# The gap between router and first expert of layer 0: rows scaled on ScalarE, shifts added at the copy out, first expert chunk ahead of a branch

## The chip, the cores and the metric

One core of a Trainium2 chip runs the whole program. The metric is the device time of one execution in microseconds (us). The kernel before takes 929.15 us (median of 3 runs, 928.97 to 929.91).

## The reference, cut to what matters

Two layers follow each other. Each has mixers (pooling, attention, a Fourier mix and an output projection), and after these a mixture of experts. The part that the change touches is the entry to the experts of layer 0, where 256 latent and 256 context tokens go through together:

```python
h2  = (rms_norm(x,  norm2_g[l]) * (1.0 + sc2) + sh2).reshape(B * N, D)
h2c = (rms_norm(xc, norm2_g[l]) * (1.0 + cs2) + ch2).reshape(B * L, D)
out = hier_moe(jnp.concatenate([h2, h2c], axis=0), *moe_args)

def hier_moe(h, w_grp, b_grp, w_rtr, b_rtr, w_gate, w_up, w_down):
    p_grp = softmax(h @ w_grp + b_grp);  pg, g = top_k(p_grp, 1)      # one of 4 groups
    logits = (h @ w_rtr + b_rtr) of that group
    pe, ie = top_k(softmax(logits), 2)                                # two of its 4 experts
    y = sum over experts e of gate[:, e] * (silu(h @ w_gate[e]) * (h @ w_up[e])) @ w_down[e]
```

The row scale of the norm (one number per token, `rs` below) multiplies a row, and the shift (`sh2` for latent, `ch2` for context tokens) is added to it. The factor (1 + scale) and the norm's weight are columns' factors and are in the tile `xt` already.

## The kernel before, in words

**Weights.** Nearly all DMA traffic is weights. `load` (L108) issues 2 MB transfers on SyncE's queue (SP) into a ring of five tiles and one further slot, in the order in which they are used. A load waits until TensorE (PE) has read the tile that it replaces. The experts are taken in four quads of four. For a quad, four chunks of `wg`, four of `wu` and then those of `wd` are used, 2 MB each.

**From the residual to the router.** When the last output projection is done, `Router` has the scaled residual transposed (L725) into `xt`: two tiles (halves of the 1024 columns) of 4 token tiles x 512. `rs` is the reciprocal of the root mean square (L278). `Route.choose` (L775 to L820) makes logits, top-1 and top-2 choices on VectorE (DVE), and counts the tokens of each expert with two sets of four small matmuls (L810, L812). `arrange` (L822 to L858) chooses the order of the quads and writes `plan`, a row of integers in which `more[q]` says whether an expert of quad q has more than 64 pairs. `slots` (L869 to L882) ends in `vec`, the two slot numbers of each token.

**Between the router and the experts.** `h2` (L745 to L752) scales each half row of `xt` by `rs` on ScalarE (ACT) and adds the shift, which stands in `room`, on GpSimd (POOL); seven of the eight half rows go that way, one is made on VectorE (L749). `split` (L115) makes of each half row a rounded part `h2h` (a cast on ScalarE) and the rest `h2l` (a subtraction on VectorE or GpSimd). Both halves of `xt` are written to DRAM (`h2d`, L1423, ScalarE's queue, 1 MB each); later quads fetch their rows from there (L1089, indirect DMAs on GpSimd's queue). `one_hots` (L1011 to L1020, pinned at L89) makes four 128x384 tiles, one for each token tile, with ones where a token's slot number is.

**Gather and branch.** `gather` (L1026 to L1044) multiplies `h2h` and `h2l` with the one-hots and so gets `XT`, the tokens of quad 0 by slot: 256 columns, 64 for each of four experts. The products are copied out by ScalarE and VectorE (L1040) in turn. Only then comes a branch (L1446) on `more[0]`, around a gather of 128 further columns for experts with more than 64 pairs. In these data it is not taken for quad 0. All engines read `plan` for it (L866). The first expert chunk (L1136) follows the branch. 8 matmuls belong to one chunk (two steps of four experts); the trace shows two records for most of them. Branches at L1146 stand around the columns beyond 64.

**Behind it.** VectorE makes diagonal tiles (`dg`, L287) which PE turns into rows that are the same on all partitions (`spread`, L288). ScalarE copies these out as `bc` and `bg` (L1162). From `bc` VectorE makes the slots' token lists (L1072 to L1084) and gates (L1122). GpSimd fetches rows of later quads by these lists. PE transposes them (L171), and ScalarE (L1102) or VectorE (L1104) copies the transposes into `XT`.

**Order.** Each engine takes its instructions in the order in which a list scheduler has laid them out from the written order; instructions marked as pinned keep the written order among themselves.

## Time and profile before

| | |
|---|---|
| median of 3 runs | 929.15 us (928.97 to 929.91) |
| the profiled execution | 929.26 us, span 927.4 us |
| PE busy | 865.7 us, 93% of the span |
| DVE, ACT, POOL busy | 409.9, 265.9, 64.5 us |
| mean DMA rate | 310 GB/s |
| mean granted PE clock | 0.979 of full speed |

PE is busy nearly all of the time and ends last, so that idle time of PE, or time at the lower of its two clocks, is what can be won. In the page's row of 40 slices PE's digits are 8 or 9 in nearly all slices behind the first; a 5 in the eleventh slice (231.9 to 255.0 us) is the largest hole. The granted clock, a row of nines, has a 6 in the same slice, an 8 further on and a 9 else. Times in the rows below are us from the start of the span. A row of a time line has start, duration, engine, line and what is written from what; a bracket at its end says how long the engine was idle before it and what ended that.

### The profile page before, as it was taken

How to read it: one execution, taken by the hardware profiler on the slowest of the kernel's cores; microseconds unless marked ns; L12 is line 12 of the kernel's file. 1: busy time of each engine (PE TensorE's matmuls, PEld its weight loads, DVE VectorE, ACT ScalarE, POOL GpSimd, SP SyncE). 2: the span in 40 equal slices, each digit the busy share in tenths (PEclk: the TensorE clock that was granted, in tenths of full speed). 3: DMA queues.
4: the chain of work that ended last, by engine and by line, in shares of the span. 5: the costliest groups of instructions: out<-in, count | busy, mean ns of one | idle time of the engine just before them, and what ended most of it. 6: DMA issues, size and time to landing. Idle time of an engine off the chain costs nothing. (4 is left out here: it accounts for less than half of the span.)

```text
span 927.4 us, 13199 instructions
## 1 busy us (share of the span) xinstructions
PE 865.7 (93%) x5078; PEld 478.1 (52%) x5078; DVE 409.9 (44%) x1028; ACT 265.9 (29%) x579; POOL 64.5 (7%) x74
## 2 busy tenths in 40 slices
PE   3899999999589999999999989989999999979998
PEld 2588676776353332442344357756973444434435
DVE  1467677633975230332221148877555241222212
ACT  3344667424320100110011055466422011100101
POOL 1000000001410030012000020000000000000000
PEclk9999999999699999999999998999999999989999
DMA  9645753744979999759958953985978999999981
GB/s 359 277 177 207 290 214 137 281 182 160 357 269 429 426 370 423 306 211 363 426 211 334 382 216 117 412 357 199 366 304 313 430 424 428 428 410 427 428 288 47
DMA packets 33826, 287.14 MB, mean 310 GB/s; under 512 B 3533, under 2 KB 13389, under 8 KB 17105
## 3 DMA queue, kind: packets, MB, share of 16 engines
q1 hardware_dynamic: 29168, 276.94, 74.3%
q0 software_dynamic: 1696, 5.79, 1.6%
q10 hardware_dynamic: 2880, 3.35, 1.0%
q8 instruction: 49, 0.80, 0.3%
q14 instruction: 33, 0.26, 0.1%
HBM read 282.90 MB, written 3.16 MB: 308 GB/s over the span
## 5 line engine op out<-in xcount | busy, mean ns | idle before, releaser
L1136 PE MATMUL acc<-w,XT 128*64 128x512 f32 (+1 forms) x768 | 171.3, 604 | 9.1 <-PEq L950 5.5
L1136 PE MATMUL aux<-w,XT 128*64 128x512 f32 (+1 forms) x512 | 109.1, 593 | 0.7 <-PEq L1146 0.7
L1136 PEld LDWEIGHTS acc<-w,XT 128*64 128x64 f32 (+1 forms) x768 | 51.5, 134 | 108.0 <-issue 103.8
L1136 PEld LDWEIGHTS aux<-w,XT 128*64 128x64 f32 (+1 forms) x512 | 33.6, 130 | 66.1 <-issue 65.3
L1136 PE MATMUL acc<-w,x 128*64 128x512 f32 (+2 forms) x272 | 55.3, 575 | 2.9 <-PEq L1146 2.3
L192 PE MATMUL aux<-w,c 128*32 128x512 f32 x368 | 49.5, 657 | 0.0
L1229 DVE SCALAR_TENSOR_TENSOR sg<-aux,gt,sg 128x512 f32<-128x512 f32 x12 | 9.0, 750 | 82.1 <-PE aux L1136 81.4
L115 DVE TENSOR_TENSOR wl<-w,wh 128x768 fp32r<-128x768 f32 (+2 forms) x48 | 43.8, 955 | 3.1 <-ACT wh L115 2.7
L1255 DVE TENSOR_TENSOR ol<-acc,oh 128x512 fp32r<-128x512 f32 (+1 forms) x25 | 15.7, 627 | 57.2 <-ACT oh L1254 57.0
L137 PE MATMUL acc<-wh,hh 128*128 128x512 f32 x96 | 38.3, 399 | 2.2 <-ACT hh L300 2.2
L1254 ACT CAST oh<-acc 128x512 fp32r<-128x512 f32 (+1 forms) x25 | 13.4, 534 | 94.0 <-PE acc L1136 93.9
L115 ACT CAST wh<-w 128x768 fp32r<-128x768 f32 (+2 forms) x48 | 37.5, 831 | 7.9 <-DMA w<-w_out 3.8
L138 PE MATMUL acc<-wl,hh 128*128 128x512 f32 x96 | 37.9, 394 | 0.0
L139 PE MATMUL acc<-wh,hl 128*128 128x512 f32 x96 | 37.8, 393 | 0.0
L1194 ACT ACTIVATE sg<-acc 128x512 f32<-128x512 f32 x16 | 9.4, 597 | 87.0 <-PE acc L1136 87.0
L525 ACT ACTIVATE pr<-acc,soft 128x512 f32<-128x512 f32 (+1 forms) x48 | 29.4, 619 | 11.7 <-DVE soft L522 11.7
L1136 PEld LDWEIGHTS acc<-w,x 128*64 128x64 f32 (+1 forms) x272 | 15.6, 130 | 32.6 <-issue 31.6
L1136 PE MATMUL aux<-w,aT 128*64 128x512 f32 (+2 forms) x192 | 29.1, 453 | 0.0
L1136 PE MATMUL acc<-w,aT 128*64 128x512 f32 (+1 forms) x160 | 28.8, 511 | 0.2 <-DVE aT L1226 0.2
L574 PE MATMUL aux<-pT,vt 128*64 128x128 f32 x320 | 27.3, 281 | 0.4 <-ACT pT L549 0.2
L1102 ACT COPY XT<-tmp 128x512 f32<-128x512 f32 x6 | 3.5, 585 | 81.6 <-PE tmp L171 81.6
L1292 DVE SCALAR_TENSOR_TENSOR xl<-tmp,modT,xl 128x256 f32<-128x256 f32 x24 | 11.2, 481 | 33.2 <-PE tmp L1272 33.0
(329 smaller groups left out, 1581.7 us busy)
## 6 DMA issues: line engine op xcount, KB each, us to landing
w<-wg SPq DMA_DIRECT2D x32, 2048.0 KB, 13.1
w<-wu SPq DMA_DIRECT2D x32, 2048.0 KB, 11.5
w<-wd SPq DMA_DIRECT2D x29, 2048.0 KB, 12.0
w<-w_mod SPq DMA_DIRECT2D x23, 2048.0 KB, 12.6
w<-w_out SPq DMA_DIRECT2D x4, 2048.0 KB, 8.3
w<-wd SPq DMA_DIRECT2D x6, 1024.0 KB, 13.4
w<-w_qkv SPq DMA_DIRECT2D x3, 1536.0 KB, 8.3
w<-w_pf SPq DMA_DIRECT2D x2, 2048.0 KB, 7.9
```

What stands on the lines that cost most here:

```text
L115: return S.copy(hi, x), eng.tensor_tensor(lo, x, hi.bitcast(F32), op=ALU.subtract)
L137: PE.matmul(out, lhs[0], rhs[0], start=start, stop=False, skip_group_check=True)
L138: PE.matmul(out, lhs[0], rhs[1], start=False, stop=False, skip_group_check=True)
L139: PE.matmul(out, lhs[1], rhs[0], start=False, stop=stop, skip_group_check=True)
L192: mm = PE.matmul(m[32 * j:32 * j + 32, :], sc2[:, k, :], w[:, kk, j * 512:(j + 1) * 512], start=(ch == chs[0] and kk == 0), stop=(ch == ch ...
L525: S.activation(pr[e], sp[e], AF.Exp, bias=nm[:, e:e + 1], scale=SCALE, accum_out=sums[:, e:e + 1])
L574: PE.matmul(o[e * 64:(e + 1) * 64, c * P:(c + 1) * P], vt[:, k0 + m, e * 64:(e + 1) * 64], pTs[e * nk + m], start=(m == 0), stop=(m == nk ...
L1136: PE.matmul(o, lh, r, start=(k == 0), stop=(k == last_k), skip_group_check=True)
L1194: S.activation(t, ga[st], AF.Silu)
L1254: S.copy(oh, da[st][:, c0:c1])
L1255: V.tensor_tensor(ol, da[st][:, c0:c1], oh.bitcast(F32), op=ALU.subtract)
L1292: V.scalar_tensor_tensor(x, y[:, s * N:(s + 1) * N], g, x, op0=ALU.mult, op1=ALU.add)
```

## The change

The rows of layer 0 are no longer shifted before the gather. `Router.high` makes `h2h` = `xt` x `rs` directly on ScalarE (8 ACTIVATE of 512 columns), and `Router.low` makes `h2l` = `xt` x `rs` - `h2h` on VectorE. The lower parts are written between the one-hots, which are 256 wide (the 128 further columns are made only in the branch), and the token tiles go in the order 2, 3, 0, 1. In the gather, eight matmuls each follow one token tile and part. Two matmuls with `ones` over the one-hots of the context tiles (2, 3) count whether a slot's token is a context token (`cb`). At the copy out ScalarE writes `XT` = `cb` x `dk` + shift, where `dk` is the difference of the two shifts by column, and VectorE adds the gathered product. The first expert chunk stands ahead of the branch (renamed L1487; the chunk's matmuls are at L1096). Rows for DRAM are made behind that: `rows` scales them by `rs` without the latent shift; context rows get the difference of shifts `ds`, which GpSimd has made earlier, two halves. The two writes of `h2d` are on GpSimd's queue. Rows fetched for later quads get the latent shift when their transposes are copied into `XT`: four ScalarE instructions of 128 columns (L1154) in place of one copy of 512, or one VectorE addition in place of a copy. Pools are renamed (`low`) so that tiles live long enough.

```diff
-        def h2(self, tt, i, rs, eng):
-            x = self.xt[i][:, tt, :]
-            sh = self.sh[:, tt // 2, i * 512:(i + 1) * 512]
...
-                S.activation(x, x, AF.Copy, scale=rs[:, tt:tt + 1])
-                G.tensor_tensor(x, x, sh, op=ALU.add)
+        def high(self, rs):
+            self.h = [self.keep.tile([P, self.nt, D], F32R, tag="h" + x, name="h2" + x, bufs=1) for x in "hl"]
+            for tt in self.turns:
+                for i, x in enumerate(self.xt):
+                    S.activation(self.h[0][:, tt, i * 512:(i + 1) * 512], x[:, tt, :], AF.Copy, scale=rs[:, tt:tt + 1])
+
+        def low(self, tt, rs):
+            for i, x in enumerate(self.xt):
+                h, o = [h[:, tt, i * 512:(i + 1) * 512] for h in self.h]
+                tc.keep_in_program_order(V.scalar_tensor_tensor(o, x[:, tt, :], rs[:, tt:tt + 1], h.bitcast(F32),
+                                                                op0=ALU.mult, op1=ALU.subtract))
+
+        def rows(self, rs):
+            for i, x in enumerate(self.xt):
+                for tt in range(self.nt):
+                    if tt < 2:
+                        S.activation(x[:, tt, :], x[:, tt, :], AF.Copy, scale=rs[:, tt:tt + 1])
+                    else:
+                        tc.keep_in_program_order(V.scalar_tensor_tensor(x[:, tt, :], x[:, tt, :], rs[:, tt:tt + 1], self.ds[i],
+                                                                        op0=ALU.mult, op1=ALU.add))
+                G.dma_start(h2d.rearrange("(t p) c -> p t c", p=P)[:, :, i * 512:(i + 1) * 512], x)
+
+        def gather(self, c0, c1, OH, XT, bank, banks):
...
+            for n, (tt, part) in enumerate(((a, 0), (b, 0), (a, 1), (c, 0), (b, 1), (d, 0), (c, 1), (d, 1))):
+                for k, y in enumerate(outs):
+                    PE.matmul(y, self.h[part][:, tt, k * P:(k + 1) * P], OH[tt][:, c0:c1],
+                              start=(n == 0 and k % k1 == 0), stop=(n == 7), skip_group_check=True)
+                if n == 1:
+
+                    for t in (a, b):
+                        PE.matmul(cb[:, 0:W], ones, OH[t][:, c0:c1].bitcast(F32), start=(t == a), stop=(t == b))
+            for k in range(KD):
+                S.activation(XT[:, k, c0:c1], cb[:, 0:W], AF.Identity, scale=self.dk[:, k:k + 1], bias=modT[0][:, 24 + k, 0:1])
+            for k, y in enumerate(outs):
+                V.tensor_tensor(XT[:, k, c0:c1], XT[:, k, c0:c1], y, op=ALU.add)
...
                     if st % 2:
-                        S.copy(d, s_)
+                        for c in range(4):
+                            S.activation(d[:, c, :], s_[:, c, :], AF.Identity, bias=modT[0][:, 24 + i * 4 + c, 0:1])
                     else:
-                        V.tensor_copy(d, s_)
+                        V.tensor_tensor(d, s_, modT[0][:, 24 + i * 4:28 + i * 4, 0:1].to_broadcast([P, 4, P]), op=ALU.add)
...
+            rt.gather(0, 256, OH, XT, tmp, [acc] * 4)
+            drain(filler)
+
+            w = ahead.pop(0)
+            begun = [acc() for _ in range(3)], []
+            for kk in range(2):
+                step(kk, KD - 1, XT[:, kk, :], w[:, kk], begun[0])
+                begun[1].append((kk, KD - 1, XT[:, kk, :], w[:, kk], begun[0]))
+            rt.rows(rs)
+            place, more = ro.order()
+            with tc.If(more[0] > 0):
...
-                for tt in range(nt):
-                    rt.h2(tt, 0, rs, G)
...
-                    nc.scalar.dma_start(h2d.rearrange("(t p) c -> p t c", p=P)[:, :, i * 512:(i + 1) * 512], rt.xt[i])
```

What VectorE has in its row from the end of `vec` on, before: one-hots of 384 columns, the lower parts by subtraction.

```order
L89 TENSOR_REDUCE vec<-rw 128x8
L115 TENSOR_TENSOR h2l<-xt,h2h 128x512
L89 TENSOR_SCALAR sj<-names,vec 128x384
L89 SCALAR_TENSOR_TENSOR OH<-names,vec,sj 128x384
L89 TENSOR_SCALAR sj<-names,vec 128x384
```

The same place of the changed kernel.

```order
L89 TENSOR_REDUCE vec<-rw 128x8
L89 TENSOR_SCALAR sj<-names,vec 128x256
L89 SCALAR_TENSOR_TENSOR OH<-names,vec,sj 128x256
L89 TENSOR_SCALAR sj<-names,vec 128x256
L89 SCALAR_TENSOR_TENSOR OH<-names,vec,sj 128x256
L767 SCALAR_TENSOR_TENSOR h2l<-xt,rs,h2h 128x512 x2
L89 TENSOR_SCALAR sj<-names,vec 128x256
L89 SCALAR_TENSOR_TENSOR OH<-names,vec,sj 128x256
L767 SCALAR_TENSOR_TENSOR h2l<-xt,rs,h2h 128x512 x2
L89 TENSOR_SCALAR sj<-names,vec 128x256
L89 SCALAR_TENSOR_TENSOR OH<-names,vec,sj 128x256
L767 SCALAR_TENSOR_TENSOR h2l<-xt,rs,h2h 128x512 x4
```

All eight lower parts now stand behind the first one-hots, each two of them reading what ScalarE wrote.

PE from the end of the gather to the first expert chunks, before (the matmuls between the branch's two rows run only where it is taken).

```order
L171 MATMUL aux<-co,ms 128x128 x4
L1036 MATMUL acc<-OH,h2h 128x256 x4
L1036 MATMUL acc<-OH,h2l 128x256 x4
L866 TENSOR_LOAD plan
L1446 COMPARE_AND_BRANCH
...
L1446 UNCONDITIONAL_BRANCH x2
L1136 MATMUL acc<-w,XT 64x512 x8
L288 MATMUL acc<-dg,co 128x128
```

The same place of the changed kernel.

```order
L791 MATMUL acc<-OH,h2l 128x256 x16
L171 MATMUL aux<-co,ms 128x128 x4
L1096 MATMUL acc<-w,XT 64x512 x13
L914 TENSOR_LOAD plan
L1487 COMPARE_AND_BRANCH
...
L1487 UNCONDITIONAL_BRANCH x2
L1096 MATMUL acc<-w,XT 64x512 x9
L985 MATMUL tmp<-small,co 128x1
L1096 MATMUL acc<-w,XT 64x512 x3
L288 MATMUL acc<-dg,co 128x128 x8
L1190 COMPARE_AND_BRANCH
```

Thirteen expert matmuls, which are chunk 0 and five of chunk 1, moved ahead of the load of `plan` and the branch, and twelve more stand ahead of the first `spread`. The second `spread` (eight matmuls at L288) stands behind 39 of the quad's 64 gate and up matmuls, where before its two halves stood behind 21 and 23 of them.

GpSimd's row, from the load of the shifts on, before and after; a bracket holds the counters that an instruction waits for.

```order
L663 DMA room<-shd 128x2048 [waits DVE_49,DMASW0_49,PE_49,DMASW1_49,Activation_49,Pool_49]
L261 TENSOR_TENSOR part<-part,sq 128x512 [waits PE_49,Activation_49]
L261 TENSOR_TENSOR part<-part,sq 128x512 [waits Activation_49] x2
L752 TENSOR_TENSOR xt<-xt,room 128x512 [waits DMASW2_49,Activation_49]
L752 TENSOR_TENSOR xt<-xt,room 128x512 [waits Activation_49] x6
L115 TENSOR_TENSOR h2l<-xt,h2h 128x512 [waits PE_49,Activation_49]
L115 TENSOR_TENSOR h2l<-xt,h2h 128x512 [waits Activation_49]
L866 TENSOR_LOAD plan [waits DVE_49]
```

```order
L668 DMA ds<-shd 128x512 [waits PE_49]
L669 TENSOR_TENSOR ds<-ds,room 128x512 [waits DMASW4_49]
L261 TENSOR_TENSOR part<-part,sq 128x512 [waits Activation_49] x3
L778 DMA h2d<-xt 128x4x512 [waits DVE_49,Activation_49] x2
L914 TENSOR_LOAD plan [waits DVE_49]
```

GpSimd's nine tensor operations of this place are gone, and the two writes of `h2d` stand there, ahead of its load of `plan`. Before, ScalarE's `COPY bc<-acc` waited for the second write of `h2d` on its own queue (`DMAHW2_49`); now it waits for the one on GpSimd's (`DMASW6_49`), because `bc` lies where `xt` was:

```order
L774 ACTIVATE xt<-xt,rs 128x512 [waits DVE_49]
L914 TENSOR_LOAD plan [waits DVE_49]
L1487 COMPARE_AND_BRANCH
...
L89 ACT_TABLE_LOAD
L89 ACTIVATE small<-small 128x16 [waits DVE_49] x2
L1495 DMA gd<-small 128x4x4 [waits DMAHW4_49,DVE_49]
L1206 COPY bc<-acc 128x512 [waits DMASW6_49,PE_49,Activation_49]
```

## Rows read from the trace of the kernel before

**Rows 1.** Stretches: busy us (records) of PE, PEld, DVE, ACT, POOL, clock, DMA share, GB/s.
```profile
242.47:248.39 5.92, 0.00 (x1) 0.03 (x1) 5.75 (x16) 0.00 (x0) 0.81 (x1) 0.50 1.04 406
248.39:253.61 5.22, 5.22 (x23) 5.11 (x24) 4.72 (x14) 0.85 (x2) 0.00 (x0) 0.50 0.46 180
261.20:296.45 35.25, 33.89 (x162) 13.65 (x162) 23.80 (x72) 5.03 (x8) 3.21 (x3) 1.00 0.85 340
```

**Rows 2.** PE's time line from the router's counts to the first spread and beyond.
```profile
238.48 0.28 PE L810 MATMUL tmp<-chosen,count 128*128 128x16 bf16 x4 [4.12 <-DVE chosen L804]
...
248.39 3.16 PE L1036 MATMUL acc<-OH,h2h 128*128 128x256 f32 x12 [5.92 <-DVE OH L89]
...
261.20 3.65 PE L1136 MATMUL acc<-w,XT 128*64 128x512 f32 x16 [2.04 <-ACTq L1446]
...
274.10 1.16 PE L288 MATMUL acc<-dg,co 128*128 128x128 f32 x8
```

**Rows 3.** POOL's time line beside the router.
```profile
231.51 9.32 POOL L752 TENSOR_TENSOR xt<-xt,room 128x512 f32<-128x512 f32 x7 [10.88 <-ACT xt L751]
```

**Rows 4.** DVE's time line in layer 0, from the choices to `vec`.
```profile
231.33 0.49 DVE L791 TENSOR_TENSOR rw<-small 128x320 f32<-128x320 f32 x1
231.74 1.56 DVE L792 TENSOR_TENSOR rw<-small 128x320 f32<-128x320 f32 x1
...
243.55 0.17 DVE L89 TENSOR_REDUCE rw<-rw 128x4 f32<-128x16 f32 x1
...
246.38 0.28 DVE L89 TENSOR_REDUCE vec<-rw 128x8 f32<-128x128 f32 x1
```

**Rows 5.** DVE's time line at the same place of layer 1.
```profile
684.84 0.32 DVE L791 TENSOR_TENSOR rw<-small 128x160 f32<-128x160 f32 x1
...
688.30 0.35 DVE L89 TENSOR_SCALAR sj<-co,vec 128x256 f32<-128x256 f32 x1
...
689.10 0.35 DVE L89 TENSOR_SCALAR sj<-co,vec 128x256 f32<-128x256 f32 x1
```

**Rows 6.** The gather's line alone in two stretches: PE, PEld, clock, DMA share, GB/s.
```profile
248.39:252.85 4.46, 4.46 (x20) 4.35 (x21) 0.50 0.54 211
255.21:257.51 2.30, 2.30 (x22) 2.30 (x20) 1.00 0.64 269
```

**Rows 7.** DVE's time line from the slots' lists to the second spread and on.
```profile
267.39 0.49 DVE L1072 TENSOR_SCALAR sj<-bc,co 128x512 f32<-128x512 f32 x1 [0.73 <-ACT bc L1162]
...
273.63 1.45 DVE L287 TENSOR_SCALAR dg<-co,vec 128x128 f32<-128x128 f32 x7
...
277.79 1.41 DVE L1073 SCALAR_TENSOR_TENSOR SS<-bc,co,sj 128x512 fp32r<-128x512 f32 x2
```

**Rows 8.** ACT's time line: scaling of rows, a copy of 256 and one of 512 columns.
```profile
230.71 4.40 ACT L751 ACTIVATE xt<-xt,rs 128x512 f32<-128x512 f32 x7 [0.24 <-DVE rs L278]
...
259.20 0.37 ACT L1040 COPY XT<-acc 128x256 f32<-128x256 f32 x1 [1.14 <-PE acc L1036]
...
305.15 0.58 ACT L1102 COPY XT<-tmp 128x512 f32<-128x512 f32 x1 [22.73 <-PE tmp L171]
```

**Rows 9.** The page's list of DMA issues: KB each, median us from issue to landing.
```profile
w<-wu SPq DMA_DIRECT2D x32, 2048.0 KB, 11.5
...
h2d<-xt ACTq DMA_DIRECT2D x2, 1024.0 KB, 16.1
...
room<-shd POOLq DMA_DIRECT2D x1, 1024.0 KB, 6.9
```

**Rows 10.** POOL's time line, the issue of the indirect fetches.
```profile
271.10 1.31 POOL L1089 DMA_INDIRECT xg<-h2d,ii  x1 [27.82 <-DVE SS L1073]
272.71 0.96 POOL L1089 DMA_INDIRECT xg<-h2d,ii  x1 [0.30 <-DVE SS L1073]
```

**Rows 11.** A stretch in which the second write and one weight load shared the DMA engines.
```profile
256.00:262.00 6.00, 3.96 (x31) 3.30 (x32) 3.29 (x15) 2.24 (x4) 0.00 (x0) 1.00 0.98 360
```

**Rows 12.** What SyncE's queue waits for from 260 to 371 us: total, times, longest.
```profile
SPq L108 <- PE acc L1136: 47.7, 9, 11.3
```

More of the change, by code (lines that the diff above doesn't have):

```diff
@@ new lines, in gather @@
+        def gather(self, c0, c1, OH, XT, bank, banks):
+            W = c1 - c0
+            k1 = 512 // W
+            cb = bank()
+            ys = [b() for b in banks]
+            outs = [ys[k // k1][:, k % k1 * W:k % k1 * W + W] for k in range(KD)]
+            a, b, c, d = self.turns
+            first = True
+            for n, (tt, part) in enumerate(((a, 0), (b, 0), (a, 1), (c, 0), (b, 1), (d, 0), (c, 1), (d, 1))):
[9 more added lines that the diff above has]
+                V.tensor_tensor(XT[:, k, c0:c1], XT[:, k, c0:c1], y, op=ALU.add)
@@ L1044, in gather, with step, experts @@
                     V.tensor_scalar(XT[:, k, c0:c1], y[:, :W], sh[k], None, op0=ALU.add)
-    def experts(l, nt, h2, vec, gov, fv, place, more, XT, xpool, pool, where, last):
+    def step(k, last_k, lhs, w, out, third=False):
+        for j in range(4):
+            o, c0, m = (out[2][32 * j:32 * j + 32, :], 256 + 32 * j, 32) if third else (
+                out[j // 2][j % 2 * 64:j % 2 * 64 + 64, :], j * 64, 64)
+            PE.matmul(o, lhs[:, c0:c0 + m], w[:, j, :], start=(k == 0), stop=(k == last_k), skip_group_check=True)
+    def experts(l, nt, h2, vec, gov, fv, place, more, XT, xpool, pool, where, last, begun):
         n = nt * P
@@ L1171, in experts @@
             quad[0] = q
-            ga = [acc() for _ in range(nst)]
+            ga, held = begun if begun and q == 0 else ([acc() for _ in range(nst)], [])
             if l == 0:
@@ L1175, in experts @@
             for ch in range(4):
-                w = ahead.pop(0) if ahead else weights(a["wg"][l, place[q], ch])
-                drain(tiles([(ch * 2 + kk, XT[:, ch * 2 + kk, :], w[:, kk]) for kk in range(2)], KD - 1, ga,
-                            ch % 2 == 0))
+                if not begun or q or ch:
+                    w = ahead.pop(0) if ahead else weights(a["wg"][l, place[q], ch])
+                    drain(tiles([(ch * 2 + kk, XT[:, ch * 2 + kk, :], w[:, kk]) for kk in range(2)], KD - 1, ga,
+                                ch % 2 == 0))
                 if ch == 0:
@@ new lines, in build @@
+                OH = {}
+                a_, b_, c_, d_ = rt.turns
+                for tt, low_part in ((a_, 0), (b_, 0), (a_, 1), (c_, 0), (b_, 1), (d_, 0), (c_, 1), (d_, 1)):
+                    if low_part:
+                        rt.low(tt, rs)
+                    else:
+                        OH[tt] = one_hot(tt, 0, 256, **hot)
+                drain(ro.plans)
+            else:
+                OH = one_hots(nt, W, names, ro.vec, keep, ("pT", "s512"), T, 4, F32, pinned(V))
+            next(filler, None)
@@ L1445, in build @@
-            if l == 0:
-                with tc.If(more[0] > 0):
-                    gather(nt, 256, W, OH, h2, XT, [acc])
-            fv = ro.beyond()
-            vec, gov = ro.vec, ro.gov
-            keep_stack.close()
-            with phase(f"ex{l}") as pool:
-                where = itertools.cycle([ring] * 5 + ([spare] * EXTRA + early if l else slot0))
-                nxt = experts(l, nt, None if l == 0 else h2, vec, gov, fv, place, more, XT, hp, pool, where, l == L - 1)
+            place, more = range(4), None
@@ L1454, in build @@
+        fv = ro.beyond()
+        vec, gov = ro.vec, ro.gov
+        keep_stack.close()
+        with phase(f"ex{l}") as pool:
+            where = itertools.cycle([ring] * 5 + ([spare] * EXTRA + early if l else slot0))
+            nxt = experts(l, nt, None if l == 0 else h2, vec, gov, fv, place, more, XT, hp, pool, where, l == L - 1, begun)
+        hp_stack.close()
         rp_stack.close()
```

151 lines of the change are left out of this document (74 added, 77 removed).

## The prediction

> **What bounds the kernel now.** I read the page's 40 slices first: PE is busy in 93% of the span, its largest hole is the slice from 231.9 to 255.0 us, and the granted clock dips in the same slice. Then I went through that stretch by windows and time lines. The reader is to see three things. PE twice has nothing to do because VectorE is late: 4.12 us until `chosen` is there, 5.92 us until the first one-hot is [rows 2]. In the stretch of the second wait the DMA engines run at 406 GB/s, so data are no lack [rows 1]. The gather then begins at the lower clock (0.50, 1.2 GHz), after PE had stood idle: a matmul takes 4.46 / 20 = 0.223 us there and 2.30 / 20 = 0.115 us (by its weight loads) at 2.4 GHz [rows 6]. And PE waits 2.04 us for the branch before the first expert chunk at 261.20 [rows 2]. From there to 296.45, the end of quad 0's gate and up products, PE works 33.89 of 35.25 us [rows 1]. So what counts is how early the first expert chunk starts, and how much of that is handed back before 296.45.
>
> VectorE is late for a reason that stands in its own rows. While GpSimd adds shifts (231.51 to 240.83, [rows 3]), operations of VectorE are stretched: L791, which begins before, takes 0.49 us, and L792 of the same shape takes 1.56; a 128x16 reduction after GpSimd has ended takes 0.17 [rows 4].
>
> **The change part by part.** The sum is made against the profiled execution, 929.26 us (span 927.4), which lies 0.1 above the median.
>
> *GpSimd leaves the router's chain.* The chain from L791 (231.33) to `vec` (246.38 + 0.28 = 246.66) took 15.3 us [rows 4]. Layer 1 runs it with half the columns and GpSimd idle: 684.84 to 688.30, 3.46 us [rows 5]. Layer 0 also has `arrange` in the chain: seven small operations, at 0.17 plus a gap of 0.03 about 1.4 us. Lower bound 3.46 + 1.4 = 4.9, were width free; upper bound 2 x 3.46 + 1.4 = 8.3. L791 takes 0.32 us with 160 columns and 0.49 with 320, and the small ones hardly change, so I take 6.0 (nearer to the lower end): `vec` at 237.35, **9.3 us earlier**. PE's fillers still end 4.12 us before 238.48 [rows 2], at about 234.35, when `chosen` is ready at the same time, so the counts cost no more than some tenths. ScalarE's eight scalings, 4.40 / 7 = 0.63 us each from 230.71 on [rows 8], end near 235.8, ahead of their readers.
>
> *One-hots and lower parts.* A one-hot of 256 columns comes every 0.80 us (688.30 to 689.10, [rows 5]). The lower part is a SCALAR_TENSOR_TENSOR on 512 columns like L1073, 1.41 us for two [rows 7], 0.66 to 0.70 each. 4 x 0.80 + 8 x 0.66 = 8.5: the last is ready at 245.9. The gather takes what is there, 8 matmuls (0.92 us at full clock) behind each. At full clock throughout it would end at 246.8. PE would be idle for some 1.5 us ahead of the gather where it was for 5.92, but nothing shows that the clock stays. If it starts at 0.50 at 238.15 and rises 5.2 us later, as it did from 248.39 to 253.61 [rows 1], 23 matmuls are done by 243.4 and the other 41 take 4.7 us: 248.1. With idle pieces that delay the rise, 250. I take 248.1. Two counts with `ones` and four transposes lie between, and VectorE's additions to the first two columns' tiles take about 0.4 us each, half of a one-hot's two instructions; the first expert chunk has its start at 248.55, **12.65 us earlier** than 261.20 (bounds 11 to 14).
>
> *What is handed back before 296.45.* (a) The branch is now behind 13 expert matmuls instead of ahead of them, and all engines still read `plan`. It cost 2.04 us [rows 2], part of which was waiting for ScalarE's table load; bounds 0 and 2.04, I take 1.0. (b) After the branch VectorE makes its gates first and `dg` later. VectorE's additions, `modT` and four rows for DRAM (4 x 0.7) end near 254; the gate operations and `dg` follow, ready at 260.5 to 262, while PE, after 25 matmuls of 0.456 (3.65 / 8, [rows 2]) and the branch, comes at about 261. I take 0.9, bounds 0 and 1.5. Together 1.9: the up products end at 248.55 + 35.25 + 1.9 = 285.7, **10.75 us earlier**.
>
> *The second spread* waits for `bc`, and `bc` now waits for the second write of `h2d` on GpSimd's queue. The rows for it are done near 254.1 and its issue follows at once. No row shows this write on this queue. 1 MB on GpSimd's queue took 6.9 us (`room`, a read), 1 MB of `h2d` on ScalarE's queue 16.1 [rows 9]: landing between 261.0 and 270.2. The load wu1, which goes out when `plan` is there (some 250), shares the engines. Both writes and it are 4.2 MB; at the 360 GB/s of a stretch where two such shared them [rows 11], that is 11.7 us from about 251 on, so I take 263, nearer to the lower end since the loads that crowded the first write of before (406 GB/s, [rows 1]) are not there. `dg` of the second spread came 6.0 us (273.37 or so) after the start of L1072 at 267.39 and the seven others by 7.7 [rows 7]; so 269.6 to 271.3. PE reaches that spread after 39 x 0.456 = 17.8 us, one spread (2.3, two like the one at 274.10, [rows 2]), the branch 1.0 and three small ones at 0.5: 248.55 + 22.6 = 271.2. It is just hidden: cost 0, and if this cover goes each us costs one.
>
> A page bears on this. GpSimd's issue of an indirect fetch took 1.31 us with VectorE busy and 0.96 a little later [rows 10], a difference of 0.35. The Trainium skill, SBUF — State Buffer (section "SBUF: two separate sides"), says that a DMA issued from GpSimd's queue can't have its descriptors written while VectorE holds the port pair that the two share, with about 3.1 us in place of 0.62; it advises ScalarE's or SyncE's queue, so it speaks against this move. By its figures each write is up to 2.5 us later, `bc` 265.5, and the sum would come out 1 to 2.5 us higher (an estimate); the row shows a seventh of that.
>
> *Copies with shift in later quads.* Quads 1 to 3 get their fetched rows by two ScalarE turns each that were one copy of 0.58 and are four instructions of 128 columns; 512 columns take 0.58 and 256 take 0.37 [rows 8], by which 128 would take 0.26 to 0.37, so 1.0 to 1.5 a turn, 0.4 to 0.9 more. Six turns: 3 at the middle if every one is on the path; but ScalarE had been idle for 22.73 us ahead of the copy shown, so most are hidden. VectorE's copies become additions on the same columns. I take **+1.0**, bounds 0 and 3.
>
> *GpSimd's differences of shifts* (two operations of some 1.3 us like those in rows 3) come long before, beside a stretch where VectorE is not late; I take 0, at most 1.
>
> Sum: 929.26 - 10.75 + 1.0 = 919.5. With the bounds of the terms: 917 to 922.5.
>
> **The rivals.**
>
> *Forecast (919.5).* As above. Against the shift going on to the end speaks only that DMA could bound behind it; SyncE's loads wait for PE 47.7 us in nine waits between 260 and 371 [rows 12], so the loads follow PE and not the other way.
>
> *B: the writes land late, 926.* If the second write needs the 16.1 us of its row [rows 9], it lands at 270.2. VectorE starts at 270.9 and ends the spread's `dg` by 278.6; PE has 25 matmuls (11.4), the last of the spread and a branch behind it, so up products end near 292.5, 4 us early: 929.26 - 4 + 1 = 926. For it: the row is that of the same bytes. Against it: that write went beside loads at 406 GB/s.
>
> *C: slower, 935.* The spread that PE does behind 25 matmuls is followed by branches behind which three 2 MB loads are free to go, at about 263.7 (248.55 + 11.4 + 2.3 + 1.0 + 0.5). If the second write is unfinished then, that is, if it takes over 9.6 us from its issue at 254.1, it shares the engines with 6 MB. By the first write's row a 1 MB write beside loads takes the time of the loads: 6.3 MB at 406 GB/s (15.5 us): `bc` at some 280, up products at 280 + 7.7 + 14 = 301.5, 5 us later than before: 929.26 + 5 + 1 = 935. For it: the margin between 263 and 263.7 is under a microsecond, and there are two prices, 6.9 and 16.1, around the point that decides. Against it: a write that is nearly done loses little, so the full price needs a write that has barely begun by then.
>
> *D: downstream hands it back, 927.* The three loads go out at 263.7 in place of 267.6 (261.20 + 3.65 + 2.3 + 0.5), 4 us earlier, while PE is 10.75 earlier; 6 to 7 us of lead are used up, and if the lead of the loads (a 2 MB load takes 11.5 us from issue to landing, [rows 9]) is smaller than that, PE waits for weights and the gain shrinks to that of the loads, 4 less 1: 926 to 928. Against it: the same waits [rows 12].
>
> *E: it does more, 916.* The chain at its lower bound and the clock at 2.4 GHz all through the gather: 1.1 + 1.3 us more, and no cost in later quads (1.0): 916.
>
> *F: it doesn't do what it says.* VectorE was stretched by something other than GpSimd, and `vec` comes no earlier than 242; then 5 us less of gain, and 924.5.
>
> **How the numbers follow.** Forecast 0.60, B 0.13, C 0.09, D 0.08, E 0.07, F 0.03. Predicted is 919.5. From 915.5 to 927.3 lie all of the forecast, most of E, the larger part of B, half of D, and F, somewhat over 8 in 10 (the forecast's own range is 917 to 922.5). A measurement of this kernel can tell 0.2%, 1.9 us, from no change. Faster than 927.3: 0.60 + 0.07 + 0.03 + 0.11 of B + 0.04 of D = 0.85. Within 0.2%: 0.02 of B, 0.04 of D and 0.02 of a mild C, 0.08. Slower: the rest of C, 0.07.
>
> **What would show it.** Right: L792 at about 0.5 us, `vec` at 236 to 239; the gather's first matmul by 239; first expert chunk at 247.5 to 250; landing of the second `h2d` write by 263.5; PE without a wait of over 1 us at the second spread; up products of quad 0 by 284 to 288, and the same distance from there to the end to within 1 to 3 us. Wrong: a PE wait at the second spread for `dg` with ScalarE's `bc` behind a DMA (B; if PE's waits reach 16 us, C), PE waits for weights between 265 and 380 (D), VectorE's operations still over 1 us with GpSimd idle (F). A PE clock that falls to 0.50 in the middle of the gather a second time would add up to 4 us.

## The result, and the profile after

The changed kernel takes 919.74 us (median of 4 runs, 918.36 to 920.78), beside 929.06 us before (4 runs, 928.38 to 929.91): a ratio of 0.9899, 95% interval 0.9883 to 0.9915, 9.3 us faster. The forecast was 919.5 us with a range of 915.5 to 927.3. The profiled execution is the slowest of the four, 920.78 us with a span of 919.0 (before: 929.26 and 927.4), so that its own difference is 8.5 us.

VectorE's time line of the changed kernel at the place of [rows 4], and on through the one-hots and lower parts:

```profile
231.85 0.49 DVE L839 TENSOR_TENSOR rw<-small 128x320 f32<-128x320 f32 x1
232.25 0.48 DVE L840 TENSOR_TENSOR rw<-small 128x320 f32<-128x320 f32 x1
...
237.73 0.29 DVE L89 TENSOR_REDUCE vec<-rw 128x8 f32<-128x128 f32 x1
238.05 0.35 DVE L89 TENSOR_SCALAR sj<-names,vec 128x256 f32<-128x256 f32 x1
...
243.85 2.73 DVE L767 SCALAR_TENSOR_TENSOR h2l<-xt,rs,h2h 128x512 fp32r<-128x512 f32 x4
```

The operation that took 1.56 us with GpSimd at work takes 0.48, like its twin ahead of it. The chain from there to `vec` is 6.17 us long (231.85 to 238.02) where it was 15.3. PE's time line at the place of [rows 2]:

```profile
235.02 0.26 PE L858 MATMUL tmp<-chosen,count 128*128 128x16 bf16 x4
...
239.07 2.14 PE L791 MATMUL acc<-OH,h2h 128*128 128x256 f32 x16 [1.83 <-DVE OH L89]
...
248.19 6.22 PE L1096 MATMUL acc<-w,XT 128*64 128x512 f32 x26
254.56 4.48 PE L1096 MATMUL acc<-w,XT 128*64 128x512 f32 x18
...
270.50 2.02 PE L288 MATMUL acc<-dg,co 128*128 128x128 f32 x16
...
293.07 1.06 PE L171 MATMUL tmp<-co,xg 128*128 128x128 f32 x8 [1.37 <-DMA xg<-h2d,ii]
```

The wait for `chosen` is gone, that for the first one-hot is 1.83 us instead of 5.92, there is no bracket at the first expert chunk and none at the second spread (270.50). One wait of over 1 us is new, 1.37 us for a fetch in the turn for quad 1. By stretches (columns as in [rows 1]), the gather's two halves and the stretch from the first chunk to the end of quad 0's up products:

```profile
237.70:243.00 5.30, 3.93 (x30) 3.85 (x31) 5.13 (x11) 0.89 (x2) 0.00 (x0) 1.00 1.00 430
243.00:247.66 4.66, 4.66 (x42) 4.66 (x40) 4.52 (x14) 4.66 (x11) 0.00 (x0) 1.00 0.99 425
248.19:284.50 36.31, 34.83 (x163) 13.65 (x162) 29.49 (x89) 7.05 (x11) 4.90 (x5) 1.00 0.89 349
```

The granted clock is 1.00 (2.4 GHz) in all three, while it was 0.50 from 236.55 to 253.61 before. The last lines for GpSimd and for the writes, its time line (the first answers to [rows 3]; the additions are gone) and the changed kernel's list of DMA issues (as [rows 9]):

```profile
252.29 0.79 POOL L778 DMA_DIRECT2D h2d<-xt  x1 [31.00 <-DVE xt L776]
253.59 0.76 POOL L778 DMA_DIRECT2D h2d<-xt  x1 [0.51 <-DVE small L89]
...
267.59 1.43 POOL L1140 DMA_INDIRECT xg<-h2d,ii  x1 [13.24 <-PEq L1190]
```
```profile
h2d<-xt POOLq DMA_DIRECT2D x2, 1024.0 KB, 8.6
...
xg<-h2d,ii POOLq DMA_INDIRECT x9, 16.0
```

The second write was complete at 263.33 in the trace, 9.7 us after its issue.

**Where the time went.** Start times of the same matmul can be subtracted between two traces; this difference I call the lead. Since each execution reaches the router a little earlier or later (here 0.5 us later), leads are taken from the start of the reciprocal that ends the norm (VectorE, 230.50 before, 231.01 after). The first expert chunk starts 30.70 us behind it before and 17.17 after: 13.5 us of lead. The transposes of `sg`, which follow the up products of quad 0, start 66.24 and 53.49 us behind it: 12.75. From quad 1's gate products on the lead is steady at 11.4 through quads 1 to 3. To the whole execution's 8.5 it is 2.9 from there: 0.5 for the later reciprocal, 1.5 net in layer 1 (0.7 gained by a shorter stretch at the lower clock near 550, 1.15 lost at one from 602.72 to 606.14 that the profile of before doesn't have, 1.0 lost near 810) and 0.9 in the last products. In other executions the clock's dips lie elsewhere, and the four runs differ by 2.4 us. In the traces of the experiments below the same stretch, from quad 1 to the end, gives anything from a gain of 0.4 us (e4) to a loss of 1.8 us (e9), but for e7, which loses in its later turns.

### The profile page after: what moved, and what is told of

Same layout as the page of the kernel before. It is cut to its first block, busy times and chain, and to the rows that moved or that the text cites. A ratio compares the mean times of both kernels' runs of the same rounds, so it can differ in the third digit from the quotient of the medians.

```text
span 919.0 us, 13230 instructions
## 1 busy us (share of the span) xinstructions
PE 862.8 (94%) x5082; PEld 477.6 (52%) x5082; DVE 406.9 (44%) x1038; ACT 270.1 (29%) x598; POOL 59.5 (6%) x71
## 5 line engine op out<-in xcount | busy, mean ns | idle before, releaser
L1096 PE MATMUL acc<-w,XT 128*64 128x512 f32 (+1 forms) x768 | 168.3, 600 | 7.4 <-PEq L998 5.8
L1096 PE MATMUL aux<-w,XT 128*64 128x512 f32 (+1 forms) x512 | 106.7, 593 | 0.6 <-PEq L1190 0.6
L1096 PEld LDWEIGHTS acc<-w,XT 128*64 128x64 f32 (+1 forms) x768 | 50.7, 133 | 106.2 <-issue 103.9
L1096 PEld LDWEIGHTS aux<-w,XT 128*64 128x64 f32 (+1 forms) x512 | 33.0, 130 | 66.0 <-issue 65.2
L1096 PE MATMUL acc<-w,x 128*64 128x512 f32 (+2 forms) x272 | 53.8, 574 | 2.6 <-PEq L1190 2.3
L192 PE MATMUL aux<-w,c 128*32 128x512 f32 x368 | 46.8, 625 | 0.0
L1096 PEld LDWEIGHTS acc<-w,x 128*64 128x64 f32 (+1 forms) x272 | 15.5, 130 | 32.4 <-issue 31.6
L1154 ACT ACTIVATE XT<-tmp,modT 128x128 f32<-128x128 f32 x24 | 7.0, 368 | 78.3 <-PE tmp L171 78.2
L1096 PE MATMUL aux<-w,aT 128*64 128x512 f32 (+2 forms) x192 | 29.1, 453 | 0.0
L1096 PE MATMUL acc<-w,aT 128*64 128x512 f32 (+1 forms) x160 | 28.8, 511 | 0.2 <-DVE aT L1271 0.2
L1082 PE MATMUL tmp<-OH,h 128*128 128x256 f32 x104 | 23.8, 383 | 2.5 <-DVE OH L1065 2.0
## 6 DMA issues: line engine op xcount, KB each, us to landing
w<-wd SPq DMA_DIRECT2D x29, 2048.0 KB, 12.9
```

Source lines behind the costliest of these rows:

```text
L192: mm = PE.matmul(m[32 * j:32 * j + 32, :], sc2[:, k, :], w[:, kk, j * 512:(j + 1) * 512], start=(ch == chs[0] and kk == 0), stop=(ch == ch ...
L1082: PE.matmul(y[:, :W], x[:, tt, k * P:(k + 1) * P], OH[tt][:, c0:c1], start=(i == 0 and tt == 0), stop=(x is h2[-1] and tt == nt - 1))
L1096: PE.matmul(o, lhs[:, c0:c0 + m], w[:, j, :], start=(k == 0), stop=(k == last_k), skip_group_check=True)
```

## The experiments

All stand against the kernel before, run on the same chip. Since a dip of the clock moves a median by a microsecond or two, I read each trace by the same three distances. They are worked out from the time lines: reciprocal to first expert chunk, reciprocal to the transposes of `sg`, and the lead behind quad 1 (at 351 us of the trace before) from the reciprocal on.

| kernel | to first chunk | to end of up products | lead in quad 1 | median us | ratio, 95% |
|---|---|---|---|---|---|
| before | 30.70 | 66.24 | 0 | 929.1 | |
| changed | 17.17 | 53.49 | 11.4 | 919.74 | 0.988 to 0.992 |
| e1, `h2d` on ScalarE's queue | 16.90 | 53.93 | 11.2 | 920.47 | 0.990 to 0.994 |
| e2, GpSimd busy | 25.87 | 62.00 | 3.6 | 925.94 | 0.996 to 0.998 |
| e3, same program as changed | 18.49 | 54.77 | 10.5 | 918.91 | 0.987 to 0.991 |
| e4, before without GpSimd's additions | 22.37 | 61.87 | 4.6 | 923.35 | 0.991 to 0.996 |
| e5, chunk behind the branch | 18.20 | 62.49 | 2.9 | 929.98 | 1.000 to 1.003 |
| e6, plain copies in the turns | 16.92 | 53.06 | 12.9 | 918.76 | 0.987 to 0.991 |
| e7, all turns by fetch | 18.50 | 54.88 | 11.3 | 920.73 | 0.989 to 0.992 |
| e8, one-hots of 384 | 18.74 | 58.37 | 7.8 | 921.51 | 0.990 to 0.993 |
| e9, first turn by fetch | 16.90 | 53.05 | 13.0 | 917.99 | 0.987 to 0.991 |
| e10, four writes | 18.49 | 56.53 | 9.5 | 920.60 | 0.989 to 0.992 |

**GpSimd put to work again.**

```diff
                     S.activation(self.h[0][:, tt, i * 512:(i + 1) * 512], x[:, tt, :], AF.Copy, scale=rs[:, tt:tt + 1])
+                    G.tensor_tensor(self.busy[:, 0:512], self.h[0][:, tt, i * 512:(i + 1) * 512].bitcast(F32), self.ds[0], op=ALU.add)
```

> The changed kernel with eight additions of 128x512 on GpSimd, each behind one of ScalarE's scalings, into a place that nobody reads; all else is as in the changed kernel. Theory (GpSimd's operations stretch VectorE's): VectorE's second and third operation of the router's chain take about 1.56 us again in place of 0.48, vec is ready 8 to 9 us later (246 to 247 instead of 238), the first expert chunk 7 to 9 us later, and the time is 926 to 929. Rival (it was the length of VectorE's list, or the wait for data, and not GpSimd): vec by 239, time within 1 us of the changed kernel's.

GpSimd's and VectorE's time lines of this kernel:

```profile
232.01 11.19 POOL L765 TENSOR_TENSOR room<-h2h,ds 128x512 f32<-128x512 f32 x8 [10.80 <-ACT h2h L764]
```
```profile
232.17 1.57 DVE L843 TENSOR_TENSOR rw<-small 128x320 f32<-128x320 f32 x1
...
235.25 0.82 DVE L847 TENSOR_REDUCE small<-rw 128x80 f32<-128x640 f32 x1
...
243.90 0.29 DVE L89 TENSOR_REDUCE vec<-rw 128x8 f32<-128x128 f32 x1
```

With additions that nobody reads, the same VectorE operation is back at 1.57 us from 0.48. The reduction, as long as without GpSimd (0.82), is not touched. `vec` is ready 13.26 us after the reciprocal (244.19 - 230.93) in place of 7.01 (238.02 - 231.01), 6.3 us later (not the 8 to 9 expected), and the gather then starts at the lower clock, which makes 8.7 us at the first chunk. The median, 925.94 us, lies just below the 926 to 929 expected. The lead falls from 11.4 to 3.6. So GpSimd's operations did stretch VectorE's, and in this place that was worth 7.8 us.

**GpSimd's additions left out, and its two lower parts given to VectorE.**

```diff
                 S.activation(x, x, AF.Copy, scale=rs[:, tt:tt + 1])
-                G.tensor_tensor(x, x, sh, op=ALU.add)
...
-                    split(*[h[:, tt, i * 512:(i + 1) * 512] for h in h2], rt.xt[i][:, tt, :], G if i and tt < 2 else V)
+                    split(*[h[:, tt, i * 512:(i + 1) * 512] for h in h2], rt.xt[i][:, tt, :], V)
```

> The kernel before with GpSimd's seven additions of the shift left out (the rows then lack the shift, so this is one part of the change alone) and its two lower parts given to VectorE; one-hots of 384 columns, the order of the gather, the branch and the queue of h2d stay as before. Theory: VectorE's chain is as short as in the changed kernel, vec at 237 to 238.5, the gather ends at 249 to 252, the first expert chunk starts 251 to 253.5 instead of 261.2, time 920 to 923. Rival: GpSimd's part is small and the gain needs the interleaved lower parts and the branch: 926 or more.

The first chunk comes 8.3 us earlier, at 252.22, inside what was expected (although 3.4 us of its gather, too, ran at a clock of 0.50), but by the end of the up products only 4.4 are left, and the median of 923.35 us is above the 920 to 923 expected. PE's time line shows where the other 3.9 went, and ScalarE's shows on what:

```profile
252.22 3.65 PE L1135 MATMUL acc<-w,XT 128*64 128x512 f32 x16 [2.03 <-ACTq L1445]
...
267.62 1.60 PE L288 MATMUL acc<-dg,co 128*128 128x128 f32 x8 [2.61 <-DVE ii L1083]
```
```profile
260.57 1.08 ACT L1161 COPY bc<-acc 128x512 f32<-128x512 f32 x2 [6.03 <-DMA h2d<-xt]
```

PE stands for 2.61 us at the second spread, for `dg`, which stands in VectorE's row behind the slots' lists, which wait for `bc`, which waits 6.03 us for the second write of `h2d`. The clock then falls to 0.50 from 268.11 to 271.53. This is rival B of the prediction, in a kernel where PE comes to the second spread behind 21 matmuls and not 39.

**The chunk written behind the branch.** The first attempt only moved the text:

```diff
-            w = ahead.pop(0)
-            begun = [acc() for _ in range(3)], []
...
                 rt.gather(256, W, OH, XT, tmp, [aux] * 2)
+            w = ahead.pop(0)
+            begun = [acc() for _ in range(3)], []
...
```

> The changed kernel with the first expert chunk written behind the branch on more[0], as it was before. Theory: PE waits for plan and the branch with nothing to do; plan is written at 248.1 in the changed kernel and the gather ends at 247.8, so the chunk starts 1 to 2 us later than 248.2, and the time is 1 to 2 us more (920.5 to 922). Rival: the branch is hidden, as its cost behind 13 matmuls was 0.15 us, and something behind it ends last: within 0.5 us.

The built program is the changed kernel's row for row: the scheduler takes the thirteen matmuls ahead of the branch from there, too, as nothing in the branch holds them. So this run tells nothing of its question. It is a second execution of the changed kernel, and a useful one: here the clock fell to 0.50 from 240.74 to 244.15, in the middle of the gather, and the gather took 10.2 us (239.86 to 250.03) where it took 8.6 at full clock. Its median of 918.91 us beside 919.74 shows how far two medians of one program lie apart.

The second attempt lets the gather inside the branch use the banks that the chunk's sums take next, and that holds the matmuls behind it:

```diff
-                rt.gather(256, W, OH, XT, tmp, [aux] * 2)
+                rt.gather(256, W, OH, XT, tmp, [acc] * 2)
+            w = ahead.pop(0)
...
```

> The changed kernel with the first expert chunk behind the branch in the built program too: the gather inside the branch takes the banks that the chunk's sums take next, so that no matmul of the quad can be put ahead. PE's order then has the branch, 8 matmuls, the first spread, its branches, and so the second spread early again, as before the change. Theory: the chunk starts 1 to 2 us later than the changed kernel's (relative to the router's start), and PE then stands at the first spread, since VectorE makes the gates ahead of dg (ready at 260 in the changed kernel, PE there at 254): 3 to 6 us of idle time, and at the second spread some more, since h2d lands at about 263. Lead over the kernel before behind quad 0 falls from 10.9 us by 5 to 8; time 923 to 927. Rival (the place of the chunk and of the spreads is of little account, GpSimd's leaving is all): within 1.5 us of the changed kernel, 918 to 921.

The first chunk starts hardly later (18.2 us behind the reciprocal instead of 17.2), and yet all of the gain is gone: 929.98 us, ratio 1.000 to 1.003, which is more than was expected (923 to 927). PE's time line, and the stretch of the lower clock:

```profile
248.27 3.65 PE L1096 MATMUL acc<-w,XT 128*64 128x512 f32 x16 [1.22 <-DVE XT L800]
256.43 0.56 PE L985 MATMUL tmp<-small,co 128*128 128x1 f32 x2 [4.51 <-DVE small L89]
257.74 3.78 PE L288 MATMUL acc<-dg,co 128*128 128x128 f32 x16 [0.75 <-DVE dg L287]
...
270.04 1.13 PE L288 MATMUL acc<-dg,co 128*128 128x128 f32 x8 [1.74 <-DVE ii L1135]
```
```profile
255.29:262.10 6.81, 4.34 (x18) 4.02 (x19) 3.66 (x23) 0.00 (x0) 0.00 (x0) 0.50 0.79 307
```

After 8 matmuls PE waits 4.51 us for VectorE's gates, 0.75 for `dg` and 1.74 at the second spread, and the clock is at 0.50 for 6.8 us. The profiled execution (927.17 us) is the fastest of its ten runs, so its lead of 2.9 us shows the least of the damage. What the change earns here is thus not the branch's 2 us but 25 expert matmuls (17 more than here) that PE can do while VectorE is at the gates and the writes are under way. And it is not earned by the place where the chunk is written: e3 and e5 differ in the banks of the gather inside the branch alone. The kernel before gives that gather the banks `acc`, in which the chunk's sums are made (L1447), and the changed one gives it `aux` (L1491). What these banks alone would bring in the kernel before was not run.

**One-hots of 384 columns in the gap.**

```diff
-                        OH[tt] = one_hot(tt, 0, 256, **hot)
+                        OH[tt] = one_hot(tt, 0, W, **hot)
```

> The changed kernel with one-hots of 384 columns in the gap, as before the change, instead of 256 with the rest in the branch. Theory: each of the four takes 0.98 us in place of 0.80, the gather follows VectorE, so its end and the first expert chunk come 0.7 us later, and 0.3 to 0.7 of it stay behind quad 0: time 919.5 to 921. Rival: the gather is bound by PE's matmuls and not by VectorE, no difference in the chunk's start over 0.2 us.

The median is 921.51 us, 0.5 above the range expected, and for another reason than the one given. The first chunk comes 1.6 us later, with a clock at 0.50 from 241.08 to 244.49. In e3, the changed kernel with such a stretch in its gather, it comes 1.3 us later, so that VectorE's longer one-hots account for 0.25 us of it and not for the 0.7 expected. But at the end of the up products 4.9 us are lost, where e3 still loses 1.3. Its PE, ScalarE and VectorE time lines:

```profile
274.41 3.03 PE L288 MATMUL acc<-dg,co 128*128 128x128 f32 x16 [2.65 <-DVE ii L1135]
```
```profile
267.33 1.07 ACT L1206 COPY bc<-acc 128x512 f32<-128x512 f32 x2 [9.62 <-DMA h2d<-xt]
```
```profile
273.89 0.37 DVE L287 TENSOR_SCALAR dg<-co,vec 128x128 f32<-128x128 f32 x1
```

The first of the three loads behind the first spread's branches in the changed kernel, from SyncE's time line:

```profile
263.31 0.33 SPq L108 DMA_DIRECT2D w<-wu  x1
```

The second write landed at 267.24, 11.2 us after its issue. The load of wu1 went out 2.5 us later than in the changed kernel, counted from the reciprocal (252.05 and 248.93; `plan` stands later in VectorE's row), and 1.2 us later than in e3; the next three loads began at 264.70, 2.5 us before the write was done. In the changed kernel the first of them went out at 263.31, just as the write was complete (263.33), and in e3 at 265.69, with the write complete at 265.66. So it is not the late chunk that costs: with the loads at the write's end e3's 1.3 us stay 1.3, and with the loads ahead of it 1.6 us become 4.9.

**The queue of the writes.**

```diff
-                G.dma_start(h2d.rearrange("(t p) c -> p t c", p=P)[:, :, i * 512:(i + 1) * 512], x)
+                nc.scalar.dma_start(h2d.rearrange("(t p) c -> p t c", p=P)[:, :, i * 512:(i + 1) * 512], x)
```

> The changed kernel with the two writes of h2d issued on ScalarE's queue again, nothing else. In the changed kernel the second write landed 9.7 us after its issue, at 263.33, 0.1 us ahead of the copy of bc, and the first spread of PE ended there anyway (263.2). Theory: the queue is of no account now, since both the issue (0.79 and 0.76 us) and the landing are hidden; landing within 1 us of before, time within 0.7 us of the changed kernel's (919 to 921). Rival (the page's rule on descriptors that GpSimd can't write while VectorE holds the port): both writes land 2 us or more earlier, bc and the fetches for quad 1 follow, PE's wait of 1.37 us for the third fetch goes, 918 or less.

Its list of DMA issues, in the window from 240 to 300 us:

```profile
h2d<-xt ACTq DMA_DIRECT2D x2, 1024.0 KB, 9.6
xg<-h2d,ii POOLq DMA_INDIRECT x3, 16.1
gd<-small ACTq DMA_DIRECT2D x1, 8.0 KB, 26.2
```

The writes land 9.6 us after their issue instead of 8.6, and the lead in quad 1 is the same to 0.2 us. But the queue is not all that differs. The scheduler has laid the work behind the branch out anew: VectorE makes `dg` in between the gates, most of the first spread is done 2.0 us earlier (260.08, 30.2 us behind the reciprocal), and PE then waits 0.94 us at the second. So the run shows that the move to the other queue gains nothing, and not what the queue alone is worth. The rule of the Trainium skill (SBUF — State Buffer, section "SBUF: two separate sides"), by which a write from GpSimd's queue would be held up by VectorE, shows in nothing here: the writes took no longer on GpSimd's queue (7.4 and 9.7 us, beside 8.9 and 10.3 on ScalarE's), and its issue instruction took 0.79 us beside an addition of VectorE and 0.76 us while VectorE had little to do (0.39 and 0.38 us on ScalarE).

**The turns for later quads.** Three kernels: copies without the shift (e6), all turns in the order of the fetches (e7), the first turn alone in that order (e9).

```diff
-                        for c in range(4):
-                            S.activation(d[:, c, :], s_[:, c, :], AF.Identity, bias=modT[0][:, 24 + i * 4 + c, 0:1])
+                        S.copy(d, s_)
...
-                        V.tensor_tensor(d, s_, modT[0][:, 24 + i * 4:28 + i * 4, 0:1].to_broadcast([P, 4, P]), op=ALU.add)
+                        V.tensor_copy(d, s_)
```

> The changed kernel with plain copies where fetched rows are turned for quads 1 to 3 (one of ScalarE on 512 columns, one of VectorE): the shift is left out for these rows. Theory: ScalarE's four instructions (1.14 and 1.38 us a turn where one copy took 0.58) lie beside PE's work; the 1.3 us that the lead loses between quad 0's up products (12.2) and quad 1 (10.9) are PE's wait for the third fetch (1.37 us), which stays. Lead behind quad 1 within 0.4 us of the changed kernel's, time 919 to 920.5. Rival (the prediction's term of +1.0 for these copies): the lead grows by 0.8 to 1.5 us.

```diff
         def turn(xg, XT):
 
-            for i in range(2):
-                for st in range(nst):
+            for st in range(nst):
+                for i in range(2):
```

> The changed kernel with the turns taken in the order of the three fetches (both halves of a fetch, then the next) instead of the first halves of all three first. PE then needs the third fetch of quad 1 some eight transposes later, 1 to 2 us. Theory: of the 1.37 us that PE waits for it (landing at 292.94, 22 us after its issue, beside weight loads) 0.7 to 1.3 go, and the lead behind quad 1 is 11.5 to 12.2 instead of 10.9; time 918.5 to 919.5. Rival: the wait moves to something else at the same point (the copies of the turns), lead unchanged.

```diff
-                turning = turn(xg, XT)
+                turning = turn(xg, XT, q == 0)      # by fetch in the first turn, by halves later
```

> The changed kernel with the order of the fetches in the first turn (for quad 1) alone; the turns for quads 2 and 3 as in the changed kernel. In e7 the first turn lost 0.1 us of the lead instead of 1.3, and the two later turns lost 1.2 each. Theory: the loss of the first turn is PE's wait for the third fetch and goes, nothing is lost later: lead behind quad 1 1.0 to 1.4 us larger than the changed kernel's, time 918 to 919. Rival: the lead is the same as the changed kernel's to 0.3 us, since the third fetch is waited for at another place.

Between the end of the up products and quad 1 the changed kernel loses 1.3 us of lead (12.75 to 11.4), e6 0.3 (13.2 to 12.9), e7 0.1 (11.36 to 11.27) and e9 0.2 (13.2 to 13.0). PE's time line of e6, then that of e9, at the place where the changed kernel waited 1.37 us:

```profile
292.52 1.06 PE L171 MATMUL tmp<-co,xg 128*128 128x128 f32 x8 [0.66 <-DMA xg<-h2d,ii]
```
```profile
291.34 0.66 PE L171 MATMUL tmp<-co,xg 128*128 128x128 f32 x4 [0.35 <-DVE XT L1157]
292.23 0.66 PE L171 MATMUL tmp<-co,xg 128*128 128x128 f32 x4 [0.23 <-ACT XT L1155]
```

In e9 there is no wait for the fetch left, and the lead is 1.6 us larger than the changed kernel's, of which 0.4 were there before the turn. e7's median, 920.73 us, is above the 918.5 to 919.5 expected: its gather had 3.4 us at 0.50, and the two later turns, which had not waited for a fetch, lost 1.2 us each. From 260 to 540 us its PE waits 2.6 us in five waits for ScalarE's copies, e9's 0.2 us. e6, whose median of 918.76 us is 0.2 below its range, is not as its theory had it: 1.0 us less is lost. 0.7 of that is the third fetch, which landed 7.73 us behind the start of the transposes of `sg` (292.39 - 284.66) instead of 8.44 (292.94 - 284.50), so up to 0.3 us is the copies' own. With 917.99 us (ratio 0.9867 to 0.9905) e9 is the fastest kernel measured; its interval overlaps that of the changed kernel, and it is by the trace and not by the medians that it is better.

**Four writes instead of two,** on top of e9:

```diff
-            for i, x in enumerate(self.xt):
-                for tt in range(self.nt):
...
+            for ctx_half in range(2):
+                for i, x in enumerate(self.xt):
...
+                    G.dma_start(out[:, ts[0]:ts[0] + 2, i * 512:(i + 1) * 512], x[:, ts[0]:ts[0] + 2, :])
```

> As e9, and h2d is written in four pieces of 0.5 MB: the latent halves as soon as ScalarE has scaled them (some 4 us before the context halves). Theory: the last write lands 1.5 to 3 us earlier than 263.3, so bc waits for the first spread alone and the fetches start up to 0.7 us earlier; the typical run gains 0.5 us or less over e9 (917.5 to 919), and the runs that are late by a write that met the three weight loads go. Rival: the rows of 2 KB or the four issues cost as much as they bring, the same landing to 0.7 us and no difference.

It did not come out: 920.60 us, and the last write landed 32.5 us behind the reciprocal (263.88) where e9's second did so at 31.9 (262.18). e9's gather was at full clock, though, and this one had 0.50 from 240.10 to 243.51; in e3 and e7, with such a stretch, the second write landed at 33.6 and 33.7, so that four writes were done some 1.1 us earlier and not 1.5 to 3. PE waited 2.29 us at the second spread:

```profile
272.20 2.02 PE L288 MATMUL acc<-dg,co 128*128 128x128 f32 x16 [2.29 <-DVE ii L1138]
```

The scheduler had laid the work behind the branch out anew: VectorE makes `dg` in between the gates, most of the first spread is done earlier (261.15, 29.8 us behind the reciprocal; 32.2 in the changed kernel), ScalarE's second copy of `bc` waits for VectorE's gates, and the second spread stands behind 35 expert matmuls instead of 39. Its `dg` came 40.3 us behind the reciprocal, as in e3 and e7 (40.3 and 40.4), so that it is PE that was there earlier. So the run tells of another order and not of four writes; what these would bring in the same order stays open.

## Why the prediction was right, point by point

**VectorE's chain.** Taken 6.0 us (bounds 4.9 and 8.3), measured 6.17. That it was GpSimd is shown by e2 from one side and e4 from the other; rival F is out.

**One-hots and lower parts.** Taken 8.5 us, measured 8.48 (from the end of `vec`, 238.02, to 246.50, where VectorE's next operation starts).

**The clock in the gather.** I took one stretch at 0.50, 1.3 us; in the profiled execution there was none, in e3, e7, e8 and e10 there was one of 3.4 us. The value lay between the two cases: in e3 the stretch cost 1.6 us of the gather's time (10.2 instead of 8.6). By it the first chunk was put 17.2 us behind VectorE's first expansion (L791, now L839); it came 16.3 behind it.

**What is handed back before the up products end.** Taken 1.9 us, measured 0.8 (36.3 from the first chunk to the transposes, 35.5 before). The branch, put at 1.0, cost 0.15: 254.41 to 254.56 in PE's time line, since `plan` was written at 248.11, 6.3 us before PE came out of its 13 matmuls. What the other 0.6 us are stays open. And `dg` was there (from 259.94 on) before PE reached the spread at 261.14.

**The second spread.** The write was forecast to land at 263, just hidden; it landed at 263.33, `dg` came from 269.98 on and PE at 270.50. From VectorE's time line:

```profile
269.98 0.37 DVE L287 TENSOR_SCALAR dg<-co,vec 128x128 f32<-128x128 f32 x1
```

The spread starts 0.52 us behind its first `dg`, just as in e8 (273.89 and 274.41), where PE stood waiting for it: nothing of the cover was left. The margin to the three loads, which the prediction put at 0.7 us, was nil (263.31 and 263.33). So rivals B and C did not happen, but e4 and e8 are B, with 2.6 us of waiting each and a clock dip behind it; e10's 2.3 us came from PE's order. Whether 0.22 was the right chance for both together can't be read from kernels that are built otherwise. C's full price of 15 us was not put to the test: in e8 the write had been under way for 8.7 us when the loads began, and the lead lost 3.3 us more than the late start of its chunk.

**The turns.** The sum had +1.0 us for ScalarE's four instructions in place of one copy. 1.3 us were lost there, but mostly to something else: the third fetch landed 22 us after its issue beside the weight loads, and PE waited 1.37 us for it. The size was right by luck, and the mechanism only in part: e9, with the same copies, has the loss gone. The prediction had no term for the fetches.

**Downstream.** D did not happen: between 260 and 540 us the changed kernel's PE waits 1.4 us for that fetch and for no load. The loads' lead was large enough. What the sum missed is the 2.4 us that the profiled execution loses behind layer 0, 1.5 in layer 1 and 0.9 at the end. It also missed 0.3 us in the turns and 0.5 that the profiled execution reached the router later. Against these stood an entry 2.0 us better than forecast (12.75 us of lead at the up products, 10.75 forecast), and a median that lies 1.0 below the profiled execution. So the mechanism was right, but that the sum is right to 0.2 us is luck: its terms were each off by up to 2.4.

**What the prediction did not see** is how the parts multiply. It costed GpSimd's leaving at 9.3 us and the moved branch at a microsecond, as if they added up. In the runs the first alone (e4) gives 4.6 us of lead, the new order with GpSimd still at work (e2) 3.6, the changed kernel without the matmuls ahead of the spreads (e5) 2.9, and all together 11.4. (The gathers of e2 and e4 ran in part at the lower clock, so their leads hold the clock's part, too.) An earlier first chunk is worth little by itself, since PE then meets the gates and the written rows 8 us earlier in its own order, and these have not become earlier by as much: in e4 the chunk came 8.3 us earlier and `bc` 5.6. What makes it worth its time is that the same edit lets 25 and 39 matmuls stand ahead of the two spreads instead of 8 and 21.

## What to carry to other kernels

When a gap in front of a bound engine is shortened, look next at the first thing behind the gap that the engine waits for and that does not move with it, and place independent work ahead of that; here the placing decided over the whole gain, and the banks of a gather in a branch decided over the placing. An operation on GpSimd that has nothing to do with the critical chain may still be its cost, when VectorE's small operations run beside it. And a transfer that must finish before a burst of loads begins has a cliff behind it: in e3 the loads began at the write's end, and a chunk that was 1.3 us late cost 1.3; in e8 they began 2.5 us ahead of it, and 1.6 us cost 4.9.

## What the runs showed of the hardware that I had not expected

- GpSimd's additions of 512 columns made some of VectorE's small operations take a full 1.1 to 1.6 us (a 16-wide addition 1.14 instead of 0.18, L89 in e2), and others nothing at all: the 640-wide reduction took 0.82 us with and without.
- An 8 KB write (`gd`) took 3.6 us to land in the changed kernel, where it was issued 3.5 us ahead of the first 2 MB load that PE's branches release (259.86 and 263.31), and 26.2 in e1, where it was issued at 263.34, behind three of them (261.23 to 262.68).
- Waits of PE of 2.6 us (e4, e8) came with 3.4 us at 0.50 of the clock close behind, and one of 4.5 us (e5) with 6.8 us that began 1.1 us before it ended. At half the rate that is up to 1.7 and 3.4 us of work, over half of the wait once more. Not every wait has that: behind e10's 2.29 us the clock stayed at 1.00.
